# Feed-forward networks that begin by tiles of tokens, and stage boundaries without GpSimd tensor work

## Chip, cores and metric

One NeuronCore of one Trainium2 chip runs the whole program. The metric is the device time of one execution in microseconds (us). Engines are named as the profile names them: PE (TensorE), DVE (VectorE), ACT (ScalarE), POOL (GpSimd), SP (the queue that issues the loads).

## What is computed

Two transformer blocks on 256 tokens of 1024 channels. The first block (two layers of attention, a mixture of experts and a gated embedding, PLE) is touched by the change only at the ends of its PLE stages. The second block is where the change lies:

```
mod = silu(c) @ w_ada + b_ada            # 9 rows of 1024: sh1, sc1, gt1, ...
n = rmsnorm(h, g_ffn1) * (1 + sc1) + sh1
h = h + 0.5 * gt1 * ((silu(n @ w1_gate) * (n @ w1_up)) @ w1_down)     # first feed-forward, D_FF = 2816
n = rmsnorm(h, g_mix) * (1 + sc2) + sh2
h = h + gt2 * hybrid_mixer(n)                                          # mixer
n = rmsnorm(h, g_ffn2) * (1 + sc3) + sh3
h = h + 0.5 * gt3 * ((silu(n @ w2_gate) * (n @ w2_up)) @ w2_down)     # second feed-forward
out = rmsnorm(h, g_final)
```

So each stage needs all of h, its sum of squares per token, a rescaling, and only then its first product.

## The kernel before

The residual h lies in SBUF as two tiles of 128 tokens by 1024 channels (t = 0, 1). Every fp32 product is made of three fp32r products of high and low parts (`mm3`, lines 304 to 306). The parts of a weight are made on the chip: `halves` (line 278) takes a unit of 1 MB, lets ACT copy its high part (line 291) and DVE or POOL subtract it (line 292), in two halves of 128x1024; four slots hold such halves. `self.aside` counts how many of the next halves POOL subtracts in DVE's place: four at the start of each of the three stages of the second block (line 392), one in each PLE stage (line 1411).

Two forms of product are used. `dense` (line 430) has tokens as output rows: 24 matmuls of 512 columns for each tile of tokens and 512 outputs; with `head` or `tail` it finishes tile 0 before tile 1, and then keeps all four halves of the weight until tile 1 has used them. `dense_T` (line 465) has the outputs transposed, with all 256 tokens as columns: 96 matmuls of 256 columns for the same work.

A stage of the second block begins in `modulated_T` (line 387). `rstd` (line 325) squares each half tile on ACT with a running sum (line 334) and takes the reciprocal root in a chain of nine small DVE instructions (lines 337, 314, 316 and 319 with 323 three times). Then `fill` gives PE some products for the modulation rows (`ada`, line 1426, matmuls on line 1447), whose result is copied out of PSUM at once (line 1450). h is transposed by PE (lines 403, 419), 1/rms is transposed and copied (lines 404/405, 420/421), and for each of 8 channel groups DVE scales, ACT adds the shift and rounds, DVE subtracts (lines 409 to 411 by tiles of tokens, the form of the mixer; 425 to 427 for all tokens at once, the form of both feed-forward networks).

`ffn` (line 486) goes through six groups of hidden columns: gate and up by `dense_T`, silu (lines 1523 to 1526), and the product with the down weights one group later, into four PSUM banks (tag a) that it takes at its start. The result reaches h in `add_gated` (lines 1482, 1483), PLE's in lines 1407 to 1409. `finish` multiplies h by the gain on POOL (line 1598), then by 1/rms on ACT and DVE (line 1601), and stores.

Nobody writes out the order by hand: the program order is a priority, and a list scheduler that runs before launch, on its own model of time, fixes each engine's queue and the use of the buffers. `ahead_by(name)` moves work forward in that priority by the number of instructions in `K["hp"]`: rstd 30, silu 200, split 60. The loads sit in SP's queue; nine units of 1 MB can be held.

Of the kernel before, what the change touches and what calls it, by code (L numbers as in the profile page):

```python
# [8 lines left out]
F32 = mybir.dt.float32  # L9
# [7 lines left out]
P = 128  # L17
T = 256
D = 1024
KT = 8  # L20
# [176 lines left out]
class Block:  # L197
    def __init__(self, ctx, tc, A, out, c_at, m_at, s_at, dbg=None):
# [14 lines left out]
        self.flip = 0  # L213
        self.waiting = []
# [109 lines left out]

    def rstd(self, tiles=(0, 1)):
# [3 lines left out]
        with self.ahead_by("rstd"):  # L329
            ss = self.stat([P, n, 2], "ss")  # L330
            for half in range(2):
                for i, t in enumerate(tiles):
                    junk = self.wk.tile([P, 512], BF16, tag="xn", name="junk", bufs=4)
                    nc.scalar.activation(junk, self.h[:, t, half * 512:(half + 1) * 512], AF.Square,
                                         accum_out=ss[:, i, half:half + 1])
            v = self.stat([P, n], "ssv")
            nc.vector.scalar_tensor_tensor(v, ss[:, :, 0], D * EPS, ss[:, :, 1], op0=OP.add, op1=OP.add)
            r = self.stat([P, n], "rstd")
            self.rsqrt(r, v, D)
# [47 lines left out]
    def modulated_T(self, gain, shift, fill, head=False):  # L387

        nc = self.nc
        r = [self.rstd([t]) for t in range(2)]  # L390
        self.fill(*fill)
        self.aside = K["aside"]
        self.fine = bool(K["fmod"])
        with self.ahead_by("mod"):
            hi, lo = self.e([P, KT, T], F32R), self.e([P, KT, T], F32R)
            if head:
                for t in range(2):
                    sl = slice(t * P, (t + 1) * P)
                    ps = [self.psb([P, 4, P]) for _ in range(2)]
# [12 lines left out]
                return hi, lo  # L412
            ps = [self.psb([P, 2, T]) for _ in range(KT // 2)]
            pr = self.psa([P, T])
            rb = self.wk.tile([P, T], F32, tag="xn", name="rbc", bufs=4)
            for t in range(2):
                sl = slice(t * P, (t + 1) * P)
                for kk in range(KT):
                    nc.tensor.transpose(ps[kk // 2][:, kk % 2, sl], self.h[:, t, kk * P:(kk + 1) * P], self.ident)
                nc.tensor.transpose(pr[:, sl], r[t].to_broadcast([P, P]), self.ident)  # L420
                nc.vector.tensor_copy(rb[:, sl], pr[:, sl])
            for kk in range(KT):
                f = self.wk.tile([P, T], F32, tag="xn", name="xn", bufs=4)
                g, b = gain[:, kk:kk + 1], shift[:, kk:kk + 1]
                nc.vector.scalar_tensor_tensor(f, ps[kk // 2][:, kk % 2], g, rb, op0=OP.mult, op1=OP.mult)
                nc.scalar.activation(hi[:, kk], f, AF.Identity, bias=b)  # L426
                nc.vector.scalar_tensor_tensor(lo[:, kk], f, b, hi[:, kk], op0=OP.add, op1=OP.subtract)  # L427
# [968 lines left out]
    def ple(self, i):  # L1396
# [7 lines left out]
        def put(ci, t, ps):  # L1404
# [4 lines left out]
            nc.vector.tensor_tensor(self.h[:, t, sl], self.h[:, t, sl], g, op=OP.add)  # L1409

        self.aside = K["aside_ple"]
# [14 lines left out]
    def ada(self, n, psum):  # L1426
# [23 lines left out]
        self.copy(rows, ps)  # L1450
# [17 lines left out]
    def add_gated(self, i):  # L1468
# [10 lines left out]
        def put(ci, t, ps):  # L1479
# [3 lines left out]
            self.nc.vector.tensor_tensor(self.h[:, t, sl], self.h[:, t, sl], y, op=OP.add)  # L1483
        return put

    def ffn(self, i, name):
        nc = self.nc
        x = self.modulated_T(self.mods[:, 3 * i + 1], self.mods[:, 3 * i], ("ffn", i))
        acc = [[self.psa([P, 512]) for _ in range(2)] for _ in range(2)]
        off, pending, done = 0, None, 0  # L1490
# [20 lines left out]
        for gi, n in enumerate(FF_GROUPS):  # L1511
            both = self.e([P, 2, 4, T], F32R)
            hT = (both[:, 0], both[:, 1])
            banks = []
            for _ in range(2):
                off = self.dense_T(x, name, n, lambda b, ps: banks.append(ps), off)
            self.ada_put()
            nb = n // 2
# [8 lines left out]
            if pending:  # L1527
                down(*pending)
# [138 lines left out]
```

## Time and profile before

| | us |
|---|---|
| median of 3 runs (1133.64 to 1138.91) | 1136.24 |
| the profiled execution, its own time | 1136.35 |
| its span, first to last instruction | 1134.2 |
| PE busy | 1066.5 (94%) |
| DVE busy | 690.4 (61%) |
| ACT busy | 517.9 (46%) |
| POOL busy | 77.2 (7%) |

2.15 us of the profiled execution lie outside its span. "Busy" counts the time in which an engine executes something, at whatever clock; PE's granted clock is a row of its own (1.00 is 2.4 GHz, 0.50 is 1.2 GHz). A row of the timeline gives start, length, engine, line, operation, what it writes and reads, the count of merged instructions, and in brackets how long the engine was idle before, with what ended that.

### The profile page before, as it was taken

To read this page: it belongs to the slowest core of one execution; us is meant where nothing else is said; L and a number is where in the kernel's file an instruction comes from. 1 tells how busy PE (TensorE), PEld (TensorE's weight loads), DVE (VectorE), ACT (ScalarE), POOL (GpSimd) and SP (SyncE) were. 2 spreads that over 40 slices of the span, in tenths; PEclk is the share of its full clock that TensorE was granted. 3 is DMA by queue.
4 is the path that set the end of the run, shared out by engine and by line. 5 is a ranking of instruction groups with operands and counts; after the bars stand their busy time and mean duration, and the time that the engine had idled before them with its cause. 6 is when DMAs were issued, how large, how long until landed. Compare 5 with 4: busy or idle time off the path is not lost.

```text
span 1134.2 us, 18483 instructions
## 1 busy us (share of the span) xinstructions
PE 1066.5 (94%) x7133; PEld 829.5 (73%) x7133; DVE 690.4 (61%) x1672; ACT 517.9 (46%) x995; POOL 77.2 (7%) x61
## 2 busy tenths in 40 slices
PE   7999999999889999899987999999989979999995
PEld 6885547765467667556545999899779659999994
DVE  6696873644479965544367557554675755554555
ACT  5445573422357774231255444343545644444443
POOL 3000000210100002100003000000300030000001
PEclk9998999999999999999998999999999989999998
DMA  9756755789975494799976447755665344454401
GB/s 371 282 203 262 296 223 210 269 340 413 411 300 185 149 382 180 263 386 365 402 277 260 143 159 252 270 179 186 222 270 186 112 185 149 175 186 160 143 26 38
DMA packets 46509, 268.58 MB, mean 237 GB/s; under 512 B 5328, under 2 KB 7120, under 8 KB 20432
## 3 DMA queue, kind: packets, MB, share of 16 engines
q1 hardware_dynamic: 46416, 267.34, 62.3%
q8 instruction: 58, 0.95, 0.3%
q14 instruction: 35, 0.29, 0.1%
HBM read 266.27 MB, written 1.05 MB: 236 GB/s over the span
## 4 chain that ended last, share of the span: by engine, by line
PE 45%; DVE 6%; DMA 1%; ACT 1%; issue 0%; DVEq 0%; ACTq 0%
PE b L305 8%; PE b L304 8%; PE b L306 8%; PE a L304 5%; PE a L306 5%; PE a L305 5%; DVE h L1483 1%; DMA raw<-in_w_ada 1%; PE a L1054 1%; DVE w L1482 1%; PE b L1460 1%; DVE nq L319 1%; PE a L1094 1%; DVE lo L292 0%; PE b L1447 0%; DVE rstd L323 0%
## 5 line engine op out<-in xcount | busy, mean ns | idle before, releaser
L292 DVE TENSOR_TENSOR lo<-raw,hi 128x1024 fp32r<-128x1024 f32 (+2 forms) x220 | 255.6, 1163 | 223.7 <-ACT hi L291 217.9
L291 ACT ACTIVATE hi<-raw 128x1024 fp32r<-128x1024 f32 (+2 forms) x234 | 235.3, 1009 | 284.6 <-PE b L305 143.5
L304 PE MATMUL b<-e,hi 128*128 128x256 f32 x768 | 219.4, 287 | 2.9 <-ACT e L426 2.9
L305 PE MATMUL b<-e,hi 128*128 128x256 f32 x768 | 219.1, 286 | 0.1
L306 PE MATMUL b<-e,lo 128*128 128x256 f32 x768 | 218.6, 285 | 0.0
L305 PE MATMUL a<-lo,e 128*128 128x512 f32 (+2 forms) x512 | 198.2, 388 | 0.0
L304 PE MATMUL a<-hi,e 128*128 128x512 f32 (+2 forms) x512 | 197.0, 393 | 1.2 <-ACT e L410 0.7
L306 PE MATMUL a<-hi,e 128*128 128x512 f32 (+2 forms) x512 | 194.8, 388 | 0.0
L304 PEld LDWEIGHTS b<-e,hi 128*128 128x128 f32 x768 | 149.3, 195 | 4.6 <-ACT e L426 3.5
L305 PEld LDWEIGHTS b<-e,hi 128*128 128x128 f32 x768 | 149.3, 195 | 1.0 <-DVE e L427 0.7
L306 PEld LDWEIGHTS b<-e,lo 128*128 128x128 f32 x768 | 149.1, 194 | 0.0
L304 PEld LDWEIGHTS a<-hi,e 128*128 128x128 f32 x512 | 97.1, 190 | 24.8 <-issue 2.8
L306 PEld LDWEIGHTS a<-hi,e 128*128 128x128 f32 x512 | 96.4, 189 | 20.1 <-DVE e L365 0.8
L305 PEld LDWEIGHTS a<-lo,e 128*128 128x128 f32 x512 | 97.2, 190 | 18.5 <-issue 0.3
L1054 PE MATMUL a<-raw,e 128*32 128x256 f32 x832 | 68.3, 383 | 1.1 <-DVEq L1291 0.8
L1107 PE MATMUL a<-w,GT 128*128 128x512 f32 x128 | 38.4, 419 | 7.7 <-ACT w L1097 3.8
L579 ACT ACTIVATE p<-p,m 128x128 f32<-128x128 f32 (+1 forms) x96 | 42.6, 450 | 6.4 <-DVE m L574 6.2
L1054 PEld LDWEIGHTS a<-raw,e 128*32 128x32 f32 x832 | 28.4, 109 | 23.4 <-issue 5.9
L292 POOL TENSOR_TENSOR lo<-raw,hi 128x1024 fp32r<-128x1024 f32 (+1 forms) x14 | 32.8, 2355 | 160.5 <-ACT hi L291 159.5
L484 DVE TENSOR_TENSOR h<-h,a 128x512 f32<-128x512 f32 x48 | 31.8, 683 | 18.2 <-PE a L1107 12.8
L1033 PE MATMUL b<-G,e 128*128 128x256 f32 x256 | 37.0, 302 | 4.7 <-DVE G L1002 4.6
L1107 PEld LDWEIGHTS a<-w,GT 128*128 128x128 f32 x128 | 21.7, 188 | 26.7 <-ACT w L1097 9.0
(322 smaller groups left out, 1419.1 us busy)
## 6 DMA issues: line engine op xcount, KB each, us to landing
raw<-in_ffn SPq DMA_DIRECT2D x62, 1024.0 KB, 4.8
raw<-in_moe_gu SPq DMA_DIRECT2D x52, 1024.0 KB, 7.4
raw<-in_w_ada SPq DMA_DIRECT2D x36, 1024.0 KB, 5.0
wd<-in_moe_dn SPq DMA_DIRECT2D x64, 512.0 KB, 7.6
raw<-in_w_gate SPq DMA_DIRECT2D x8, 1024.0 KB, 12.8
raw<-in_w_m_in SPq DMA_DIRECT2D x8, 1024.0 KB, 5.6
raw<-in_w_a_in SPq DMA_DIRECT2D x7, 1024.0 KB, 10.4
e<-in_moe_gu SPq DMA_DIRECT2D x6, 1024.0 KB, 10.1
```

The lines of the kernel that those rows point to most:

```text
L291: nc.scalar.activation(hi[:, sl], raw[:, at], AF.Copy)
L292: eng.tensor_tensor(lo[:, sl], raw[:, at], hi[:, sl], op=OP.subtract)
L304: mm(out, l[0], r[0], start=start, stop=False, **kw)
L305: mm(out, l[0], r[1], start=False, stop=False, **kw)
L306: mm(out, l[1], r[0], start=False, stop=stop, **kw)
L319: nc.vector.scalar_tensor_tensor(q, y, h, y, op0=OP.mult, op1=OP.mult)
L484: self.nc.vector.tensor_tensor(self.h[:, t, sl], self.h[:, t, sl], ps, op=OP.add)
L579: nc.scalar.activation(p, p, AF.Exp, bias=m[:, i:i + 1], scale=-1.0, accum_out=den[:, i:i + 1])
L1033: nc.tensor.matmul(ps[:, j], xh[part][:, t, sl], G[:, t], start=(t + j + part == 0), stop=(t + part == 2), skip_group_check=True)
L1054: nc.tensor.matmul(pgs[pp][32 * x:32 * x + 32], xg[:, k, o:o + 32], wg[kk][:, x], start=(k == 0), stop=(k == KT - 1))
L1094: nc.tensor.matmul(py[32 * x:32 * x + 32], hT[:, 32 * x:32 * x + 32], wd[2 * n + x // 2][:, x % 2], start=True, stop=True)
L1107: nc.tensor.matmul(ps, GT[:, t * P:(t + 1) * P], y[:, n * 512:(n + 1) * 512], start=(b == 0), stop=(b == len(back) - 1))
```

## The change

Each rstd of the stage starts and of the end uses sums of squares that are collected when a half tile of h gets its last value. Both feed-forward networks use the norm by tiles of tokens, and compute gate and up of the first group by `dense` with `head`, transposing the product of the silu afterwards. The four accumulator banks are taken one group later. The fill of a stage start comes after tile 0's norm in program order, its results are copied behind the norm, and they lie in the banks of tag a. Nothing is put on POOL in `halves` any more, nor in `finish`. The diff, cut to its core:

```diff
+    def square(self, out, t, half):
+        junk = self.wk.tile([P, 512], BF16, tag="xn", name="junk", bufs=4)
+        self.nc.scalar.activation(junk, self.h[:, t, half * 512:(half + 1) * 512], AF.Square, accum_out=out)
+
+    def square_new(self, ci, t):
+
+        if ci + t == 0:
+            self.squares = self.stat([P, 2, 2], "squares", bufs=1)
+        with self.ahead_by("rstd"):
+            self.square(self.squares[:, t, ci:ci + 1], t, ci)
+
     def rstd(self, tiles=(0, 1)):
...
+            if self.squares is not None:
+                ss = self.squares[:, tiles[0]:tiles[0] + n]
+            else:
...
-    def modulated_T(self, gain, shift, fill, head=False):
-
-        nc = self.nc
-        r = [self.rstd([t]) for t in range(2)]
-        self.fill(*fill)
-        self.aside = K["aside"]
-        self.fine = bool(K["fmod"])
+    def modulated_T(self, gain, shift, fill, head=True):
+
+        nc = self.nc
+        hi, lo = self.e([P, KT, T], F32R), self.e([P, KT, T], F32R)
+        r = [None, None]
         with self.ahead_by("mod"):
-            hi, lo = self.e([P, KT, T], F32R), self.e([P, KT, T], F32R)
             if head:
                 for t in range(2):
                     sl = slice(t * P, (t + 1) * P)
+                    r[t] = self.rstd([t])
+                    if t:
+                        self.squares = None
+                        self.fill(*fill)
                     ps = [self.psb([P, 4, P]) for _ in range(2)]
...
-            ps = [self.psb([P, 2, T]) for _ in range(KT // 2)]
...
+        for rows, ps in self.copies:
+            self.copy(rows, ps)
+        self.copies = []
         return hi, lo
...
             nc.vector.tensor_tensor(self.h[:, t, sl], self.h[:, t, sl], g, op=OP.add)
-
-        self.aside = K["aside_ple"]
+            if i:
+                self.square_new(ci, t)
+
         self.fine = bool(K["fine"])
...
-    def ada(self, n, psum):
+    def ada(self, n, psum, later=False):
...
-        self.copy(rows, ps)
+        if later:
+            self.copies.append((rows, ps))
+        else:
+            self.copy(rows, ps)
...
             self.nc.vector.tensor_tensor(self.h[:, t, sl], self.h[:, t, sl], y, op=OP.add)
+            self.square_new(ci, t)
         return put
...
-        acc = [[self.psa([P, 512]) for _ in range(2)] for _ in range(2)]
...
-            banks = []
-            for _ in range(2):
-                off = self.dense_T(x, name, n, lambda b, ps: banks.append(ps), off)
+            banks, gates, rows = [], [], []
+            nb = n // 2
+            if gi == 0:
+                def put_up(ci, t, ps):
+                    with self.ahead_by("silu"):
+                        f = self.w4([P, 512])
+                        nc.scalar.activation(f, gates[t], AF.Tanh, scale=0.5)
+                        nc.vector.scalar_tensor_tensor(f, f, 1.0, gates[t], op0=OP.add, op1=OP.mult)
+                        nc.vector.scalar_tensor_tensor(f, f, 0.5, ps, op0=OP.mult, op1=OP.mult)
+                        rows.append(f)
+
+                off = self.dense(x, name, [512], lambda ci, t, ps: gates.append(ps), off, head=True)
+                off = self.dense(x, name, [512], put_up, off, head=True)
+                nb = 0
+                for b in range(2):
+                    with self.ahead_by("silu"):
+                        ps = self.psb([P, 2, T])
+                        for j in range(2):
+                            for t in range(2):
+                                nc.tensor.transpose(ps[:, j, t * P:(t + 1) * P],
+                                                    rows[t][:, (2 * b + j) * P:(2 * b + j + 1) * P], self.ident)
+                        self.parts(hT[0][:, 2 * b:2 * b + 2], hT[1][:, 2 * b:2 * b + 2], ps)
+            else:
+                for _ in range(2):
+                    off = self.dense_T(x, name, n, lambda b, ps: banks.append(ps), off)
...
             if pending:
+                if acc is None:
+                    acc = [[self.psa([P, 512]) for _ in range(2)] for _ in range(2)]
                 down(*pending)
...
-                nc.gpsimd.tensor_tensor(o[:, t, sl], self.h[:, t, sl], self.g_final[:, sl], op=OP.mult)
-            for half in range(2):
-                sl = slice(half * 512, half * 512 + 512)
-                self.copy(o[:, t, sl], o[:, t, sl], r)
+                nc.vector.scalar_tensor_tensor(o[:, t, sl], self.h[:, t, sl], r, self.g_final[:, sl], op0=OP.mult,
+                                               op1=OP.mult)
...
-            self.ada(n, self.psb if where.startswith("ffn") else self.psa)
+            self.ada(n, self.psb if where == "ffn0" else self.psa,
+                     where in ("ffn", "mixer"))
```

## Rows read from the trace of the kernel before

**Rows 1.** The page's busy times: us, share of the span, instructions.

```profile
PE 1066.5 (94%) x7133; PEld 829.5 (73%) x7133; DVE 690.4 (61%) x1672; ACT 517.9 (46%) x995; POOL 77.2 (7%) x61
```

**Rows 2.** Engine times by stretch; the last three columns: PE's clock, DMA share, GB/s.

```profile
607.96:620.03 12.07, 5.99 (x40) 2.65 (x40) 10.83 (x28) 4.73 (x11) 5.34 (x2) 0.82 0.91 351
620.03:634.00 13.97, 13.91 (x93) 13.62 (x94) 9.04 (x18) 6.97 (x11) 0.00 (x0) 0.79 0.31 112
817.25:827.76 10.51, 6.40 (x50) 2.78 (x50) 10.12 (x28) 4.38 (x11) 5.15 (x2) 0.98 0.97 386
827.76:842.04 14.28, 14.28 (x64) 11.95 (x65) 10.85 (x36) 8.99 (x19) 0.00 (x0) 0.90 0.56 228
919.75:931.66 11.91, 5.70 (x34) 2.69 (x33) 10.57 (x29) 4.78 (x12) 5.26 (x2) 0.78 0.88 353
931.66:945.50 13.84, 13.79 (x95) 13.49 (x96) 9.37 (x18) 6.96 (x11) 0.00 (x0) 0.82 0.15 48
1122.80:1134.20 11.40, 0.00 (x0) 0.00 (x0) 7.32 (x24) 3.15 (x8) 3.38 (x3) 0.72 0.25 92
```

**Rows 3.** Timeline, second PLE stage into the first feed-forward network.

```profile
605.34 7.96 POOL L292 TENSOR_TENSOR lo<-raw,hi 128x1024 fp32r<-128x1024 f32 x3 [0.34 <-ACT hi L291]
...
606.68 1.62 DVE L1408 SCALAR_TENSOR_TENSOR w<-w,e 128x512 f32<-128x512 f32 x1 [5.18 <-ACT w L1407]
...
607.89 2.77 PE L1447 MATMUL b<-raw,c 128*32 128x512 f32 x22
...
608.33 2.75 DVE L1409 TENSOR_TENSOR h<-h,w 128x512 f32<-128x512 f32 x1
...
611.61 2.24 DVE L1408 SCALAR_TENSOR_TENSOR w<-w,e 128x512 f32<-128x512 f32 x1
...
613.88 0.69 DVE L1409 TENSOR_TENSOR h<-h,w 128x512 f32<-128x512 f32 x1
...
614.50 0.15 DVE L337 SCALAR_TENSOR_TENSOR ssv<-ss 128x1 f32<-128x1 f32 x1
...
614.61 0.63 ACT L334 ACTIVATE junk<-h 128x512 bf16<-128x512 f32 x1 [1.67 <-DVE h L1409]
...
615.15 0.19 ACT L334 ACTIVATION_READ_ACCUMULATOR junk<-h 128x1 f32 x1
...
616.09 0.16 DVE L323 SCALAR_TENSOR_TENSOR rstd<-nq,rstd 128x1 f32<-128x1 f32 x1
...
616.81 0.29 DVE L421 COPY rbc<-a 128x128 f32<-128x128 f32 x1 [0.19 <-PE a L420]
...
618.96 1.27 DVE L425 SCALAR_TENSOR_TENSOR xn<-b,mods,rbc 128x256 f32<-128x256 f32 x3
...
620.04 0.58 PE L304 MATMUL b<-e,hi 128*128 128x256 f32 x1 [1.45 <-ACT e L426]
```

**Rows 4.** Timeline, first feed-forward network into the mixer.

```profile
813.27 0.69 DVE L1482 TENSOR_TENSOR w<-a,w 128x512 f32<-128x512 f32 x1 [5.29 <-PE a L306]
...
818.74 2.67 DVE L1483 TENSOR_TENSOR h<-h,w 128x512 f32<-128x512 f32 x1
```

**Rows 5.** Timeline of DVE, mixer into the second feed-forward network.

```profile
918.12 1.29 DVE L1482 TENSOR_TENSOR w<-a,w 128x512 f32<-128x512 f32 x2 [5.53 <-PE a L306]
...
923.33 2.83 DVE L1483 TENSOR_TENSOR h<-h,w 128x512 f32<-128x512 f32 x2
```

**Rows 6.** The chain that ended last: start, us, what (a step's pitch).

```profile
585.15 0.87 PE b L359 x8
...
605.24 0.23 PE a L304
...
638.71 0.12 PE b L305
```

**Rows 7.** DVE by line and form from 600 us on: count, busy us, mean ns.

```profile
L292 DVE TENSOR_TENSOR lo<-raw,hi 128x1024 fp32r<-128x1024 f32 x137 | 167.8, 1225 | 156.5 <-ACT hi L291 156.0
```

**Rows 8.** Timeline, the end of the program.

```profile
1130.01 0.72 ACT L261 ACTIVATE e<-e,rstd 128x512 f32<-128x512 f32 x1 [0.84 <-DVE rstd L323]
```

More of the change, by code (lines that the diff above doesn't have):

```diff
@@ L329, in rstd @@
         with self.ahead_by("rstd"):
-            ss = self.stat([P, n, 2], "ss")
-            for half in range(2):
[L332 to L335, printed above, removed]
+            if self.squares is not None:
+                ss = self.squares[:, tiles[0]:tiles[0] + n]
+            else:
+                ss = self.stat([P, n, 2], "ss")
+                for half in range(2):
+                    for i, t in enumerate(tiles):
+                        self.square(ss[:, i, half:half + 1], t, half)
             v = self.stat([P, n], "ssv")
@@ L398, in modulated_T @@
                     sl = slice(t * P, (t + 1) * P)
+                    r[t] = self.rstd([t])
+                    if t:
+                        self.squares = None
+                        self.fill(*fill)
                     ps = [self.psb([P, 4, P]) for _ in range(2)]
@@ L411, in modulated_T @@
                         nc.vector.scalar_tensor_tensor(lo[:, kk, sl], f, b, hi[:, kk, sl], op0=OP.add, op1=OP.subtract)
-                return hi, lo
-            ps = [self.psb([P, 2, T]) for _ in range(KT // 2)]
[L414 to L427, printed above, removed]
+        for rows, ps in self.copies:
+            self.copy(rows, ps)
+        self.copies = []
         return hi, lo
@@ L1488, in ffn @@
         x = self.modulated_T(self.mods[:, 3 * i + 1], self.mods[:, 3 * i], ("ffn", i))
-        acc = [[self.psa([P, 512]) for _ in range(2)] for _ in range(2)]
-        off, pending, done = 0, None, 0
+        off, pending, done, acc = 0, None, 0, None
         n_tiles = sum(FF_GROUPS)
@@ L1513, in ffn @@
             hT = (both[:, 0], both[:, 1])
-            banks = []
-            for _ in range(2):
-                off = self.dense_T(x, name, n, lambda b, ps: banks.append(ps), off)
+            banks, gates, rows = [], [], []
[22 more added lines that the diff above has]
+                    off = self.dense_T(x, name, n, lambda b, ps: banks.append(ps), off)
             self.ada_put()
-            nb = n // 2
             for b in range(nb):
@@ L1597, in finish @@
                 sl = slice(half * 512, half * 512 + 512)
-                nc.gpsimd.tensor_tensor(o[:, t, sl], self.h[:, t, sl], self.g_final[:, sl], op=OP.mult)
-            for half in range(2):
-                sl = slice(half * 512, half * 512 + 512)
-                self.copy(o[:, t, sl], o[:, t, sl], r)
+                nc.vector.scalar_tensor_tensor(o[:, t, sl], self.h[:, t, sl], r, self.g_final[:, sl], op0=OP.mult,
+                                               op1=OP.mult)
                 nc.sync.dma_start(self.out[t * P:(t + 1) * P, sl], o[:, t, sl])
```

## The prediction, made before the changed kernel was run

> **What bounds the kernel now.** I read the page's busy times first, then the engine times by stretch, then the timeline at each stage boundary, and last the chain that ended last. PE is busy 94% of the span [rows 1], so away from the boundaries only fewer or faster matmuls would help. The reader should see in the stretches that the boundaries are where it is not so. From PE's last product of one stage to its first of the next pass 12.07 us (second PLE into first feed-forward, called P), 10.51 us (into the mixer, M) and 11.91 us (into the second feed-forward, F), of which PE works 5.99, 6.40 and 5.70; after PE's last product 11.40 us remain (E) [rows 2]. The stretch behind each boundary, up to the end of its first weight matrix, runs at a mean clock of 0.79, 0.90 and 0.82 of 2.4 GHz: it begins at 1.2 GHz. What that loses is length times what is missing of 1: 13.97 x 0.21 = 2.9, 14.28 x 0.10 = 1.4, 13.84 x 0.18 = 2.5 us. The three boundaries so hold 6.1 + 4.1 + 6.2 = 16.4 us of PE idle and 6.8 us of lost clock.
>
> What fills them is the chain last product, h final, squares, reciprocal root, norm, first product. In it DVE is stretched while POOL subtracts weights: in P three instructions of 512 columns take 1.62, 2.75 and 2.24 us during POOL's 7.96, and the next, when POOL has ended at 613.30, takes 0.69 [rows 3]. In M one takes 2.67 [rows 4], with 5.15 us of POOL in that stretch [rows 2].
>
> **The parts.** Each boundary is rebuilt with the prices of [rows 3]: a DVE instruction of 512 columns 0.69 us; a square 0.63 and its read of the sum 0.19, 0.82; the root from 614.50 to 616.25, 1.75; up to the end of the copied 1/rms at 617.10, 0.85 more; from the norm's first instruction at 618.96 to the first product at 620.04, 1.1. (What lies between 617.10 and 618.96 is the second tile's root, which tile 0 need not await when the norm goes by tiles.) From a tile's squares to its first product that is 3.7 us.
>
> P. DVE does tile 0's last two instructions from 606.68 to 608.06. Tile 0's sum would be ready at 608.9; I take 609.5, since ACT has tile 1's tanh to give at the same time, and 0.5 more because the root shares DVE with tile 1's last instructions. First product at 609.5 + 0.5 + 3.7 = 613.7 instead of 620.04 [rows 3].
>
> The first matrix then goes by tiles as the mixer's does now: 14.28 us [rows 2], less 1.4 for the clock and less 16 matmuls for modulation rows that the mixer has inside (about 0.1 each, 1.6) makes 11.3. To that I add 1.2 for one weight half that DVE must now subtract while the norm needs it. End 626.2 instead of 634.00: **-7.8**.
>
> M. The norm is by tiles already. DVE needs 4 x 1.38 from 813.27, done at 818.8 instead of 821.41 [rows 4]. Tile 0's chain would allow a product near 821.8; but PE has work of its own: 32 matmuls of the fill from 817.25 at 0.126 (2.77 / 22 [rows 3]), 4.0, and eight transposes, 0.87 [rows 6]. That gives about 822.3 instead of 827.76: -5.5. With PE filled I expect no fall of the clock, -1.4; one subtraction in the way, +1.2. **-5.7**.
>
> F. DVE cannot start before 918.12, when the accumulations end nearly together [rows 5]. Three pairs of instructions end tile 0 at 922.3, its square ends at 923.1, plus 3.7 is 926.8, or 927.3 with the same 0.5 as in P; I take 927.0 against 931.66. PE has only 14 matmuls of the fill and transposes for that time, so I leave the clock low: 11.3 + 1.4 + 1.2 = 13.9, end 940.9 instead of 945.50 [rows 2]. **-4.6**.
>
> E. The last update of h starts at 1122.85, after PE's last product [rows 2]: 1.38, square 0.82, root 1.75, two scalings on DVE at 0.69 each make 1128.2; the last instruction now ends at 1130.73 [rows 8]. -2.5, less 0.5 for tile 0's root and scaling on the same DVE: **-2.0**. The stores behind it stay.
>
> What the change adds. Sixteen transposes of the silu product per network, 16 x 0.109 [rows 6] = 1.7. Up by tiles takes 48 x 0.23 = 11.0 rather than 96 x 0.12 = 11.5 [rows 6], -0.5 (gate's is in the sums above). **+2.4** for both networks. POOL's twelve subtractions of the second block cost DVE 12 x 1.23 [rows 7] = 14.7 us. Two of each four lie before the boundary, where DVE waits 5.18, 5.29 and 5.53 us for PE [rows 3 to 5]; of the others I charged one. Without that cover it would be two more per boundary, 2.5 us. The halves moved from POOL in PLE and half of the squares hide beside the products of the stage before.
>
> Edits that I cost at nothing: the copies of the fill move behind the norm (each of the price of an instruction of 512 columns at most), and what reads them, the modulation rows, waits till the first group is done; their PSUM banks are wanted next by up, eleven us after gate begins. SP's queue keeps the order of its loads, since the fill's still stand before the stage's weights; in M, where DMA is at 0.97, the first units have landed by the time of their subtraction. The accumulators move behind the first group and are first used in the second. No row shows a head pass in a network, nor two in a row; bounds: nothing, since the mixer's goes over into the next matrix at 842.04 without idle [rows 2], or a subtraction and its copy on ACT, 2.4 us, at each of four handovers, 10 us. I take nothing, the nearest row being the mixer's.
>
> **Sum.** 7.8 + 5.7 + 4.6 + 2.0 - 2.4 = 17.7. The profiled execution took 1136.35, 0.11 over the median of the runs, so this makes 1118.6. The most that the rows hold is all idle and all lost clock, 23.2, and 2.5 in E, less 2.4: 23.3, or 1113; two more for E and for stores that wait less, and the range ends at 1111.
>
> **A rule that speaks against it.** In P the clock fell between PE's last transposes and the first product: the boundary as a whole has 0.82, the stretch behind it 0.79 [rows 2], after 22 fill matmuls and then mostly transposes. The Trainium skill (TensorE: Matmul & The Clock Gate, Part 4: PE-mode transpose) says that transposes do not count as PE activity for the clock. By that rule the fill of my gaps with transposes would not hold the clock in P and M; no row here separates the two. That mechanism is rival 3.
>
> **Rivals.**
> 1. *DVE becomes the bound.* It is busy 10.83 of 12.07 us in P, 10.12 of 10.51 in M, 10.57 of 11.91 in F [rows 2]. Against it: in P 4.5 of that is stretch (6.61 less 3 x 0.69), and tile 1's root, about 2, may come after tile 0's first products, so 4.3 remain, or 5.6 with one subtraction, in the 5.7 us that I leave. For it: that is no room at all, and if the second subtraction or tile 1's root stand first, 1.2 to 2 us go at each start and as much again in the norm. I price it as half of the gain: (17.7 + 2.4) / 2 - 2.4 = 7.7, 1128.7.
> 2. *Split slots (slower).* Head passes hold all four slots of split halves until tile 1's pass. If the next matrix's halves come only after that pass, each takes ACT and then DVE (1.23 [rows 7], and ACT about as much), 2.4, where PE uses one in 6 x 0.23 = 1.4 [rows 6]: per handover 2.4 for the first and 1.0 for each of three more, 5.4, plus 1.4 for the silu's two DVE instructions at the same time; four handovers, 27 us: 1145.6. Against: the mixer hands over to its second matrix without idle (PE 14.28 of 14.28 [rows 2]). It decides from 4.4 us a handover on (17.7 / 4).
> 3. *Low clock at all three starts.* The fall that I remove in P and M stays: 2.9 + 1.4 = 4.3, 1122.9.
> 4. *The order eats it.* The scheduler's queues are fixed ahead on its own model: PE's may hold tile 1's transposes before tile 0's products, DVE's a subtraction before the puts, and other stages may shift. Then tiles first does not happen, and what the missing POOL gives is paid for by the moved subtractions: about 0 to -3, 1134.5.
>
> **Chances.** Forecast 0.52; rival 1 0.19; rival 3 0.14; rival 4 0.08; rival 2 0.07. A measurement of this kernel can tell about 0.5%, 5.7 us, from no change: 1130.5 to 1142. The forecast, rivals 1 and 3 lie below: 0.85. Rival 4 is no change, 0.08; rival 2 is slower, 0.07. To leave out no more than two in ten the range must take in rival 1 with its bounds (one unit of splitting more, 2.5): 1111 to 1131.
>
> **What would show it.** No POOL rows at line 292 or 1598; lines 1409 and 1483 at 0.69 throughout; boundary stretches, from PE's last product to its first, of about 5.7, 5.0 and 7.3 us where they are 12.07, 10.51 and 11.91. The clock behind P and M near 1.00 and behind F near 0.9. Gate and up of the first group without PE idle. Tile 0's first products ahead of tile 1's transposes in PE's timeline. I am wrong if PE idles at the handovers from gate to up, or if DVE's rows between the stages show no waiting while PE does, or if the stages before the second PLE change length.

## The result, and the profile after

The changed kernel takes 1121.6 us, the median of 4 runs (1121.3 to 1122.49); beside it the kernel before took 1137.58. The ratio is 0.9864, with a 95% interval of 0.9842 to 0.9886: faster by 1.4%, 3.0 us less than forecast and inside the range. A second series of six runs gave 1121.43 and 0.9855 (0.9825 to 0.9885).

The page's busy times after, which answer to [rows 1]:

```profile
PE 1057.6 (95%) x6957; PEld 815.0 (73%) x6957; DVE 694.9 (62%) x1720; ACT 520.1 (46%) x1009; POOL 38.9 (3%) x43
```

The engine times by stretch of the changed kernel, columns as in [rows 2]. The borders are PE's last and first main products (0.1 to 0.2 us ahead of those in [rows 2]): P, the first network, M, the mixer, F, the second network, E. In what follows a stretch between two stages is a wait, and the stage behind it a body.

```profile
605.86:616.96 11.10, 7.42 (x47) 2.65 (x47) 10.59 (x40) 5.84 (x14) 0.00 (x0) 0.85 0.61 222
616.96:810.77 193.81, 193.81 (x1297) 177.71 (x1298) 119.04 (x148) 86.62 (x107) 1.90 (x2) 1.00 0.61 218
810.77:821.54 10.77, 7.71 (x51) 3.15 (x50) 10.42 (x40) 6.33 (x15) 0.00 (x0) 0.84 0.56 206
821.54:910.79 89.25, 87.73 (x505) 73.25 (x505) 52.52 (x142) 46.28 (x79) 0.00 (x0) 1.00 0.49 180
910.79:921.00 10.21, 5.83 (x35) 3.31 (x35) 10.02 (x34) 4.96 (x13) 0.00 (x0) 0.83 0.57 207
921.00:1109.21 188.21, 188.21 (x1249) 173.68 (x1249) 107.80 (x135) 85.81 (x108) 0.00 (x0) 1.00 0.39 137
1109.21:1119.14 9.93, 0.17 (x1) 0.00 (x0) 6.61 (x25) 1.45 (x4) 0.00 (x0) 0.71 0.28 106
```

The three waits have hardly become shorter: 11.10, 10.77 and 10.21 us, where 5.7, 5.0 and 7.3 were forecast. What became shorter is the bodies behind them. Both networks have PE busy for their whole length at a clock of 1.00, and the low clock (0.85, 0.84, 0.83 in the mean) now lies inside the waits: in P it was 1.2 GHz from about 616 to 626 us before, and is so from about 612 to 615 us after, over by the first product. Cut in the same places, the profile before has 12.25 + 197.04, 10.68 + 91.91, 11.99 + 190.96 and 11.60 us. So a wait with its body got 4.38, 2.57 and 4.53 us shorter, E 1.67. The 1.93 that is left of the 15.1 lies ahead of P. Some 1.2 of it is ten of the fill's 32 products, which before ran among PLE's products (from 588.70 us on) and now stand in the wait; the rest is less than the scatter there: the kernels below whose stages up to P are alike reach it between 604.2 and 610.6 us.

What PE and DVE do in P, from the timeline after:

```profile
606.98 0.69 DVE L1410 SCALAR_TENSOR_TENSOR w<-w,e 128x512 f32<-128x512 f32 x1
...
607.73 1.23 DVE L294 TENSOR_TENSOR lo<-raw,hi 128x1024 fp32r<-128x1024 f32 x1
...
608.12 0.19 ACT L329 ACTIVATION_READ_ACCUMULATOR junk<-h 128x1 f32 x1
...
608.87 0.68 DVE L1411 TENSOR_TENSOR h<-h,w 128x512 f32<-128x512 f32 x1
609.47 0.15 DVE L351 SCALAR_TENSOR_TENSOR ssv<-squares 128x1 f32<-128x1 f32 x1
...
609.70 0.63 PE L418 MATMUL b<-consts,h 128*128 128x128 f32 x4 [1.43 <-DVE ssv L351]
611.40 0.32 PE L419 MATMUL a<-consts,rstd 128*128 128x128 f32 x1 [1.06 <-DVE rstd L325]
611.65 5.30 PE L1450 MATMUL a<-raw,c 128*32 128x512 f32 x32
616.89 0.32 PE L419 MATMUL a<-consts,rstd 128*128 128x128 f32 x1
616.96 0.48 PE L306 MATMUL a<-hi,e 128*128 128x512 f32 x1
```

DVE's instructions of 512 columns take 0.69 instead of 1.62 to 2.75 [rows 3]. Tile 0's sum of squares is read out by 608.31, but its root begins at 609.47, since DVE has a weight subtraction (607.73) and tile 1's last update in front of it: 3.6 us behind PE's last product, where the prediction had 1.5 and 0.5 more (609.5 with that product at 607.96). PE, besides, has left its 32 products of the fill (line 1450, nothing the network waits for) until tile 0's transposed 1/rms is through, and runs them at 611.65, mostly at the low clock (0.69 in the mean from 611.40 to 616.96), while the first product (line 306) stands behind them in its queue. In [rows 3] 22 of them ran at 607.89, inside the idle time. In M it is the same:

```profile
815.94 0.32 PE L419 MATMUL a<-consts,rstd 128*128 128x128 f32 x1 [1.57 <-DVE rstd L325]
816.20 5.34 PE L1450 MATMUL a<-raw,c 128*32 128x512 f32 x32
...
821.54 0.47 PE L306 MATMUL a<-hi,e 128*128 128x512 f32 x1
```

The update of h in the kernel before, DVE by line and form (count, busy us, mean ns of one, idle time before them):

```profile
L1483 DVE TENSOR_TENSOR h<-h,w 128x512 f32<-128x512 f32 x12 | 15.8, 1320 | 0.2
L1482 DVE TENSOR_TENSOR w<-a,w 128x512 f32<-128x512 f32 x12 | 8.1, 684 | 16.1 <-PE a L306 16.1
```

and after:

```profile
L1489 DVE TENSOR_TENSOR h<-h,w 128x512 f32<-128x512 f32 x12 | 8.2, 688 | 0.2
L1488 DVE TENSOR_TENSOR w<-a,w 128x512 f32<-128x512 f32 x12 | 8.1, 685 | 5.3 <-PE a L308 5.3
```

Only the addition was stretched, 1320 ns against 688; the product beside it, which reads one operand from PSUM, took 684 and 685. The Trainium skill (SBUF — State Buffer, Who interferes with whom) says that a DVE instruction with two SBUF inputs contends with a GpSimd instruction that reads SBUF; these rows agree.

### The profile page after: what moved, and what is told of

Same layout as the page of the kernel before. It is cut to its first block, busy times and chain, and to the rows that moved or that the text cites. A ratio compares the mean times of both kernels' runs of the same rounds, so it can differ in the third digit from the quotient of the medians.

```text
span 1119.1 us, 18152 instructions
## 1 busy us (share of the span) xinstructions
PE 1057.6 (95%) x6957; PEld 815.0 (73%) x6957; DVE 694.9 (62%) x1720; ACT 520.1 (46%) x1009; POOL 38.9 (3%) x43
## 4 chain that ended last, share of the span: by engine, by line
PE 46%; DVE 4%; DMA 1%; ACT 1%; issue 0%; DVEq 0%
PE b L306 7%; PE b L307 7%; PE b L308 7%; PE a L306 6%; PE a L308 6%; PE a L307 6%; DVE lo L294 1%; PE a L1450 1%; DMA raw<-in_w_ada 1%; PE a L1056 1%; DVE h L1489 1%; DVE w L1488 1%; PE b L1466 1%; ACT hi L293 1%; PE a L1096 0%
## 5 line engine op out<-in xcount | busy, mean ns | idle before, releaser
L294 DVE TENSOR_TENSOR lo<-raw,hi 128x1024 fp32r<-128x1024 f32 (+2 forms) x234 | 271.3, 1162 | 227.2 <-ACT hi L293 221.0
L307 PE MATMUL a<-lo,e 128*128 128x512 f32 (+2 forms) x576 | 222.0, 387 | 0.0
L306 PE MATMUL a<-hi,e 128*128 128x512 f32 (+2 forms) x576 | 220.6, 391 | 0.5 <-ACT e L378 0.3
L308 PE MATMUL a<-hi,e 128*128 128x512 f32 (+2 forms) x576 | 218.5, 388 | 0.0
L306 PE MATMUL b<-e,hi 128*128 128x256 f32 x640 | 181.8, 284 | 0.0
L307 PE MATMUL b<-e,hi 128*128 128x256 f32 x640 | 181.4, 283 | 0.0
L308 PE MATMUL b<-e,lo 128*128 128x256 f32 x640 | 181.2, 283 | 0.0
L306 PEld LDWEIGHTS a<-hi,e 128*128 128x128 f32 x576 | 108.8, 189 | 24.5 <-issue 1.9
L308 PEld LDWEIGHTS a<-hi,e 128*128 128x128 f32 x576 | 108.3, 189 | 21.6 <-issue 0.8
L306 PEld LDWEIGHTS b<-e,hi 128*128 128x128 f32 x640 | 123.0, 192 | 1.1 <-ACT hi L293 0.8
L307 PEld LDWEIGHTS a<-lo,e 128*128 128x128 f32 x576 | 108.8, 189 | 20.6 <-issue 0.3
L307 PEld LDWEIGHTS b<-e,hi 128*128 128x128 f32 x640 | 123.0, 192 | 0.3
L308 PEld LDWEIGHTS b<-e,lo 128*128 128x128 f32 x640 | 122.9, 192 | 0.0
L1096 PE MATMUL a<-wd,hT 128*32 128x512 f32 x256 | 41.1, 617 | 1.5 <-ACT hT L1091 1.2
```

What stands on the lines that cost most here:

```text
L294: eng.tensor_tensor(lo[:, sl], raw[:, at], hi[:, sl], op=OP.subtract)
L306: mm(out, l[0], r[0], start=start, stop=False, **kw)
L307: mm(out, l[0], r[1], start=False, stop=False, **kw)
L308: mm(out, l[1], r[0], start=False, stop=stop, **kw)
L1096: nc.tensor.matmul(py[32 * x:32 * x + 32], hT[:, 32 * x:32 * x + 32], wd[2 * n + x // 2][:, x % 2], start=True, stop=True)
```

## The experiments

Time is compared by the ratio to the kernel before on the same chip. Where it went is read from one profiled execution each, by the seven stretches (wait + body, us). The rows with a plus, both orders and one held have the fill first besides.

| kernel | P + network | M + mixer | F + network | E | sum | median | ratio (95%) |
|---|---|---|---|---|---|---|---|
| before | 12.25 + 197.04 | 10.68 + 91.91 | 11.99 + 190.96 | 11.60 | 526.4 | 1137.58 | 1 |
| changed | 11.10 + 193.81 | 10.77 + 89.25 | 10.21 + 188.21 | 9.93 | 513.3 | 1121.60 | 0.9864 (0.9842, 0.9886) |
| before, no GpSimd | 9.01 + 196.97 | 7.42 + 90.54 | 10.14 + 190.78 | 9.91 | 514.8 | 1124.09 | 0.9882 (0.9853, 0.9911) |
| GpSimd back | 12.88 + 193.79 | 14.18 + 88.35 | 12.32 + 188.19 | 9.92 | 519.6 | 1127.19 | 0.9905 (0.9869, 0.9941) |
| all tokens | 8.83 + 195.89 | 10.71 + 89.25 | 11.14 + 190.35 | 9.92 | 516.1 | 1125.67 | 0.9886 (0.9858, 0.9913) |
| fill first | 7.68 + 193.80 | 7.42 + 89.34 | 9.63 + 188.21 | 9.92 | 506.0 | 1116.81 | 0.9821 (0.9790, 0.9851) |
| fill first, again | 7.67 + 193.79 | 7.41 + 89.31 | 9.62 + 188.21 | 9.92 | 505.9 | 1119.08 | 0.9813 (0.9781, 0.9845) |
| + squares late | 13.79 + 196.18 | 13.71 + 89.00 | 15.85 + 190.25 | 9.92 | 528.7 | 1138.22 | 0.9988 (0.9968, 1.0008) |
| + copies at once | 7.67 + 195.41 | 7.42 + 89.34 | 9.71 + 189.59 | 9.93 | 509.1 | 1118.65 | 0.9818 (0.9788, 0.9849) |
| + DVE's order | 8.34 + 195.94 | 7.24 + 90.26 | 9.70 + 190.48 | 9.92 | 511.9 | 1118.75 | 0.9813 (0.9783, 0.9843) |
| root's bank | 7.93 + 196.25 | 8.93 + 90.95 | 9.93 + 189.09 | 9.94 | 513.0 | 1123.48 | 0.9864 (0.9833, 0.9896) |
| both orders | 5.88 + 197.77 | 6.36 + 91.32 | 7.52 + 190.85 | 9.92 | 509.6 | 1118.07 | 0.9812 (0.9784, 0.9839) |
| one held | 5.88 + 197.38 | 6.36 + 89.48 | 8.96 + 189.59 | 9.92 | 507.6 | 1114.64 | 0.9797 (0.9767, 0.9827) |

**The fill first.** The fill's products come ahead of the norm in program order, as before the change:

```diff
         r = [None, None]
+        self.fill(*fill)
         with self.ahead_by("mod"):
...
                         self.squares = None
-                        self.fill(*fill)
```

> The changed kernel with the fill put at the head of modulated_T, ahead of tile 0's norm in program order; its copies stay behind the norm. Theory (the fill's products, which now stand in PE's queue behind tile 0's transposed 1/rms, cost 5.3, 5.3 and 1.9 us there while PE idled 4 to 5 us before): first products come some 3.7 us earlier in P, 3.8 in M, 0.5 in F, the clock in P stays high; about 6 us less than the changed kernel, 1115 to 1117 us. Rival (the norm on DVE sets the pace anyway, the fill only filled time that the norm needs): under 2 us, 1120 to 1122.

The theory held: 1116.81, and the waits shrink by 3.4, 3.4 and 0.6 us (in P 0.9 of that is eight of the fill's products, which now run ahead of the border). The timeline of P:

```profile
605.52 2.78 PE L1450 MATMUL a<-raw,c 128*32 128x512 f32 x24
608.24 2.10 PE L418 MATMUL b<-consts,h 128*128 128x128 f32 x16
611.49 0.29 PE L419 MATMUL a<-consts,rstd 128*128 128x128 f32 x1 [1.15 <-DVE nq L321]
612.97 0.29 PE L419 MATMUL a<-consts,rstd 128*128 128x128 f32 x1 [1.19 <-ACT e L425]
613.10 0.47 PE L306 MATMUL a<-hi,e 128*128 128x512 f32 x1
```

The fill now lies where PE has nothing else, and the first product comes 7.7 us behind the last one; the prediction had 5.7 (613.7 behind 607.96). Tile 1's transposed root still stands ahead of it in PE's queue, which the prediction had not.

**GpSimd alone, both ways.** The kernel before without tensor work on GpSimd, and the changed kernel with the weight subtractions of the stage starts back on it:

```diff
-    aside=4,
+    aside=0,
...
-    aside_ple=1,
+    aside_ple=0,
```

and the gain of the last norm on DVE as in the change;

```diff
         r = [None, None]
+        self.aside = K["aside"]
...
+        self.aside = K["aside_ple"]
         self.fine = bool(K["fine"])
```

> The kernel before, with all subtractions and the final gain on VectorE and nothing else changed. Theory (GpSimd's stretching of VectorE is the larger part of what the change removes): 8 to 12 us faster than the kernel before, 1126 to 1130. Rival (the parts by tiles and by earlier squares carry the gain): 0 to 4 us faster, 1134 to 1138.

> The changed kernel with the first four weight halves of each stage of the second block, and one of each PLE stage, subtracted on GpSimd again (the end stays on VectorE). Theory (GpSimd stretches VectorE's two-operand instructions at the boundaries by some 4 us each, and VectorE takes the subtractions mostly in idle time): 7 to 11 us slower than the changed kernel, 1129 to 1133. Rival (VectorE is the bound at the boundaries, so what it gains without GpSimd it pays for the subtractions): within 2 us, 1120 to 1124.

The first came out below its theory's 1126: taking GpSimd away from the kernel before gives 13.4 us by the ratio, where the whole change gives 15.5 (0.0118 and 0.0136 of 1138.5), and 11.7 of 13.2 by the stretches. Its P and M:

```profile
606.62:615.63 9.01, 5.63 (x42) 2.64 (x41) 8.31 (x29) 4.62 (x11) 0.00 (x0) 0.94 0.96 394
...
812.60:820.02 7.42, 6.32 (x52) 2.79 (x51) 7.22 (x28) 3.91 (x9) 0.00 (x0) 1.00 0.76 282
```

Both waits are shorter than the changed kernel's. In the kernel before, the first product of all three stages waits for the norm (ACT's e, 0.70 to 1.45 us), not for a weight half, which points to the stretch of DVE's chain and not to GpSimd's own pace. The fill first, run on the same chip, is 7.3 us below this kernel (1116.81): the rest of the change is worth that much where the fill stays early, and 1.5 to 2 where it is late. Put back, GpSimd costs 5.6 us by the medians, 4.7 by the ratios and 6.4 by the stretches, between the two theories; the timeline shows the stretched instruction again (L1411 here is L1410 of the changed kernel):

```profile
605.44 5.10 POOL L294 TENSOR_TENSOR lo<-raw,hi 128x1024 fp32r<-128x1024 f32 x2
605.65 2.70 DVE L1411 SCALAR_TENSOR_TENSOR w<-w,e 128x512 f32<-128x512 f32 x1 [2.42 <-ACT w L1410]
```

The two sizes, 13.4 and 5.6, differ because the parts don't add: in E the gain of 1.7 stays in the second kernel (its last norm is not put back), and its low clock lies in the waits (0.73, 0.76, 0.72) while its bodies stay at 1.00. How much is due to each, no run separates.

**All tokens.** The networks' norm and first group for all 256 tokens at once, as before the change; the rest as changed (`head=False`, and `dense_T` for the first group).

> The changed kernel with both feed-forward networks' norm and first group for all tokens at once as before (GpSimd, squares, copies and accumulators stay as changed; the fill of the networks then stands ahead of the transposes again). Theory of the prediction (tiles first let the first product start early): 4 to 8 us slower than the changed kernel, 1126 to 1130. Rival (in the changed kernel the late fill ate that head start, and the sixteen transposes cost 1.7 us per network): within 2 us of it, or faster, 1118 to 1123.

1125.67 lies between the two. By the ratio it is 0.0022 slower than the changed kernel, which the intervals don't separate; by the stretches 2.8 us, all of it at F (3.1). At P it costs nothing (-0.2), since that form of norm also brings the fill forward (8.83). So in the kernel as changed, tiles first is worth some 3 us, and loses at P what the fill's place takes. Beside the fill first, which ran on the same chip and has the fill early in the networks too, it is worth more: 3.2 us at P and 3.7 at F by the stretches, in which 3.2 more lie at M, where this kernel is as changed; the medians are 8.9 us apart and the intervals don't meet.

**Where the fill's place comes from.** One word of the changed kernel: the transposed 1/rms goes into a bank of the transposes' pool.

```diff
-                    pr = self.psa([P, P])
+                    pr = self.psb([P, P])
```

> The changed kernel with one word altered: tile 0's and tile 1's transposed 1/rms go into a bank of the other PSUM pool (the one the transposes use), not into the pool that the modulation products and the network's products share. Theory (the products of the fill stand behind tile 0's transposed 1/rms because PSUM banks of a pool are handed out in program order, so that they wait for the bank that follows it): the fill's products move ahead of it in TensorE's order by themselves, the gaps between main products shrink from 11.1, 10.8 and 10.2 us to 7 to 8.5 at P, 7 to 8.5 at M and 9 to 10 at F, and the time falls 5 to 8 us below the changed kernel's 1121.6. Rival (it is the place in the program, which sets the priority): order and gaps stay, 1120 to 1123.

At P and F the gaps came as the theory has them, at M 0.4 longer (8.93); the time, at the changed kernel's ratio, did not. In P:

```profile
605.02 3.63 PE L1450 MATMUL a<-raw,c 128*32 128x512 f32 x30
...
611.35 0.29 PE L419 MATMUL b<-consts,rstd 128*128 128x128 f32 x1 [2.11 <-DVE nq L321]
611.48 1.20 PE L418 MATMUL b<-consts,h 128*128 128x128 f32 x8
...
612.85 0.50 PE L306 MATMUL a<-hi,e 128*128 128x512 f32 x1 [0.17 <-ACT e L425]
```

Nothing but the pool of that small tile was changed, and the fill begins 0.1 us behind the last product instead of 5.8 (605.02 after 604.92, 611.65 after 605.86): sharing a pool with the fill and the products is what held it. That banks are handed out in program order is the reading that fits; no run shows the handing out itself. The waits give back 5.3 us, and the bodies take 5.0: the products begin while tile 0's norm is still going, and at a clock of 0.98 to 0.99 in two bodies.

**Late squares, and copies at once,** both on top of the fill first: `square_new` does nothing; and `ada` is always called with `later` False.

> The kernel with the fill's products first, with the squares summed only where the 1/rms is wanted, as before the change. Theory (two squares of 0.63 us and a read of 0.19 each stand on ScalarE in front of tile 0's root, behind weight conversions of 1.05): 0.5 to 1.5 us more at each of P, M and F, and 0 to 2 at E, so 2 to 5 us more than with the early squares, 1119 to 1122. Rival (VectorE's order ends each wait later than the squares do, whichever place they have): every gap within 0.4 us, the time within 1 us of 1116.8.

> The kernel with the fill's products first, with the fill's copies issued right behind them, as before the change, not behind the norm. Theory (with the fill early, its copies are ready in the idle part of the wait and are taken there anyway): every gap within 0.7 us, the time within 1.5 us of 1116.8. Rival (copies of 0.68 us stand ahead of the root on VectorE or of the squares on ScalarE): 0.7 to 1.4 us more at P and M and 0.7 at F, 1119 to 1121.

Late squares cost far more than either theory: 1138.22, all of the change's gain. The timeline of P shows why:

```profile
620.98 0.40 ACT L425 ACTIVATE e<-xn,mods 128x128 fp32r<-128x128 f32 x1 [0.39 <-DVE xn L424]
...
621.28 0.61 ACT L329 ACTIVATE junk<-h 128x512 bf16<-128x512 f32 x1
...
621.90 0.61 ACT L329 ACTIVATE junk<-h 128x512 bf16<-128x512 f32 x1
...
624.67 0.45 PE L419 MATMUL a<-consts,rstd 128*128 128x128 f32 x1 [7.42 <-DVE rstd L325]
...
624.79 0.76 PE L306 MATMUL a<-hi,e 128*128 128x512 f32 x1
```

Tile 1's squares (line 329) stand on ACT behind seven of tile 0's eight normed blocks (line 425), its root follows them, and PE, in order, idles 7.42 us for that root with tile 0's products queued behind. So in this order, with tile 1's root queued ahead of the first product, the early squares are what lets a start by tiles work; their own 0.82 us are the small part. Late squares with that root behind the first products were not run. E is 9.92 either way: there they are worth nothing. The copies' place is worth nothing that these runs show: the waits are the same to 0.1 us, and so is the ratio to 0.0003.

**What keeps the waits above the forecast.** On top of the fill first, tile 1's root waits for tile 0's, and two weight subtractions and the fill's copies wait for four of tile 0's eight blocks (`issue_after`):

```diff
-                    r[t] = self.rstd([t])
+                    with self.tc.issue_after(self.root.ins) if t else nullcontext():
+                        r[t] = self.rstd([t])
...
-                    eng.tensor_tensor(lo[:, sl], raw[:, at], hi[:, sl], op=OP.subtract)
+                    with self.behind():
+                        eng.tensor_tensor(lo[:, sl], raw[:, at], hi[:, sl], op=OP.subtract)
```

> The kernel with the fill's products first, and besides it three things held back on VectorE at the three starts: tile 1's root until tile 0's is done, and two weight subtractions (1.22 us each) and the fill's copies (0.68) until four of tile 0's eight normed blocks are out. Theory (what keeps those gaps at 7.67, 7.41 and 9.64 us is VectorE's other work ahead of tile 0's root: 1.9 us of it at P, about 3 at M, 1.2 to 2.4 at F, and 0.6 of interleaved roots at each): gaps of 5.3 to 6.3 at P, 4.7 to 5.8 at M and 7.0 to 8.5 at F, the bodies of the stages unchanged, a span of 1104 to 1108 against 1111.4. Rival (the subtractions held back starve the first products, or another chain such as ScalarE's is as long): gaps or bodies give it back, span 1110 to 1113.

The theory fell: the waits are 8.34, 7.24 and 9.70, the bodies 5.3 longer in sum. Tile 0's transposed root came 4.6 us behind the last product (605.92) instead of 6.1, and P became longer all the same, 8.34. In this kernel and the two that follow, the lines have other numbers: L316 and L318 are main products, L432 the transposed root, L296 the weight subtraction, L270 the copy, L439 the norm's subtraction, L335 the root's last step. PE's timeline in P, with that step:

```profile
610.53 0.27 PE L432 MATMUL a<-consts,rstd 128*128 128x128 f32 x1
...
613.91 0.15 DVE L335 SCALAR_TENSOR_TENSOR rstd<-nq,rstd 128x1 f32<-128x1 f32 x1
...
614.21 0.29 PE L432 MATMUL a<-consts,rstd 128*128 128x128 f32 x1 [3.41 <-ACT e L438]
...
614.26 0.47 PE L316 MATMUL a<-hi,e 128*128 128x512 f32 x1
```

PE waits 3.41 us for tile 1's root, delayed by the edit itself and ahead of the first product in the queue (the bracket names ACT, but the root ended at 614.06). Both orders together:

> The fill's products first, the three things held back on VectorE as in the run of the vector order, and the transposed 1/rms of each tile in a bank of the transposes' pool as in the run of the root's bank. Theory (in the run of the vector order TensorE's queue held tile 1's transposed root ahead of the first product, which idled 3.41 us for it; the other bank puts that root behind the first products): the first product follows tile 0's root by about 2 us, gaps of 5.8 to 6.8 at P, 5.0 to 6.5 at M and 7.8 to 9.0 at F. The bodies are 193.8, 89.3 and 188.2 us where the clock doesn't fall and up to 2.5 more each where it falls behind the wait; so a span of 1105 to 1113, and 2 to 5 us less than the kernel with the fill's products alone first. Rival (tile 1's root, now inside the products, stops TensorE there for as long, or the clock falls at all three starts whatever the gap): the bodies give it all back, and the time is within 1.5 us of that kernel's or above it.

The gaps are those of the theory or shorter (5.88, 6.36, 7.52), 5.0 us less in sum than with the fill first; the bodies are 8.6 longer, and the time is the rival's: 1118.07, beside 1119.08 for the fill first on the same chip. One reason is a stop that the edit makes, the two held subtractions and a copy ahead of tile 0's fifth block on DVE (the next expectation calls it the seventh), and PE at that block:

```profile
612.68 2.35 DVE L296 TENSOR_TENSOR lo<-raw,hi 128x1024 fp32r<-128x1024 f32 x2
614.95 0.68 DVE L270 COPY w<-a 128x512 f32<-128x512 f32 x1
615.55 0.33 DVE L439 SCALAR_TENSOR_TENSOR e<-xn,mods,e 128x128 fp32r<-128x128 f32 x1
...
615.94 0.50 PE L318 MATMUL a<-hi,e 128*128 128x512 f32 x1 [1.50 <-DVE e L439]
```

So one subtraction only was held, behind six blocks (`2, 2` becomes `3, 1`, `kk == 3` becomes `kk == 5`), with the changed kernel beside it on the same chip:

> As the run of both orders, but only one weight subtraction is held back, and it and the fill's copies wait for six of tile 0's eight normed blocks, not four. Theory (in that run the two subtractions and a copy, 2.35 and 0.68 us, stood before tile 0's seventh block and stopped TensorE there: 1.50, 1.50 and 0.90 us of idle behind P, M and F, and slower products around them): gaps of 5.8 to 6.2 at P, 6.5 to 7.5 at M and 8.0 to 9.0 at F, bodies without those stops, a span of 1106 to 1112, and 1 to 4 us less than the run of both orders. Rival (VectorE's whole work for the norm of both tiles sets when the second tile's products can run, wherever the one subtraction stands): the idle moves to the second tile's products and the time stays within 1 us of 1118.1.

> The changed kernel itself beside the run above, on the same chip. By its first runs 1121.3 to 1122.5 with a clock of 0.985 to 0.988, a span of 1119.1 made of gaps of 11.1, 10.8 and 10.2 us and bodies of 193.8, 89.2 and 188.2: theory (its fall of the clock always lands on the fill, in the waits) the same again, 1120.5 to 1123.5, a spread under 2 us; rival (its falls reach the products in other executions, as those of the other kernels do): a spread of 4 us or more.

1114.64 (1114.0 to 1117.22) against 1121.43 (1120.5 to 1124.21): 6.8 us under the changed kernel, 22.4 under the one before: the lowest median and ratio of all, though its interval (0.9767 to 0.9827) takes in the fill first (0.9821 and 0.9813). The gaps are the theory's at P and F and 0.1 shorter at M. The changed kernel repeated itself, five of six runs within 1.4 us and one 3.7 above the lowest, between theory and rival, with its fall of the clock in the waits again (0.84, 0.84, 0.83). The stop in P is 0.52, in M none:

```profile
610.49:807.87 197.38, 196.34 (x1297) 178.67 (x1297) 123.75 (x167) 88.10 (x113) 1.90 (x2) 0.99 0.59 213
...
814.23:903.71 89.48, 87.95 (x505) 73.21 (x505) 57.21 (x161) 48.05 (x86) 0.00 (x0) 1.00 0.49 186
```

In P the first product is 1.8 us earlier than with the fill first, yet wait and body together are 1.8 longer. The traces say where that went. The 96 products of gate and up end 29.3 us behind PLE's last product, against 29.7 with the fill first, both at a clock of 1.00: 1.4 of the lead went to products that came at the norm's pace on DVE. Then PE stops at the silu's transposes, where the fill first does not:

```profile
634.41 0.44 PE L1555 MATMUL b<-consts,w 128*128 128x128 f32 x2 [0.52 <-DVE w L1544]
```

and from about 637 to 640 us its clock is 1.2 GHz (0.56 in the mean from 636.80 to 640.50), which costs some 1.6 us more.

**The fill first, again,** to see whether its clock of 1.00 holds:

> The kernel with the fill's products first once more, beside the run above. In its first profile the granted clock was 1.00 behind all three waits; its nearest neighbour, with the copies at once, has the same gaps and falls at P and F. Theory (whether the clock falls behind such a wait is chance between executions): gaps of 7.6 to 7.8, 7.3 to 7.6 and 9.5 to 9.8 again, but a low clock behind at least one of the three starts, a body or two longer by 1 to 2.5 us, median 1116 to 1119. Rival (this order of the work keeps the clock up): 1.00 in all three again, bodies of 193.8, 89.3 and 188.2, median 1113 to 1116.

Its profile repeats the first to 0.1 us. But its six executions ran at mean clocks of 0.980 to 0.993 and spans of 1110.2 to 1120.3 us, with the median, 1119.08, at the theory's upper edge: the profile is as the rival has it, the median as the theory has it. Both profiles show the good end. The stretches above are to be read as where time can go, the medians as what it takes.

## Why the prediction was right, and where its steps failed

Sign and range held; 1121.6 lies 3.0 us above the forecast and 1.3 below rival 3's 1122.9. The way there did not hold, and that the number came so near is in part luck. The three waits were to give 16.5 us and gave 2.8; the bodies were to grow by 0.8, the added transposes included, and shrank by 8.6; and 1.9 lie ahead of P. The stages before the second PLE kept their length: its first tanh begins at 596.89 us before, at 596.53 and 597.14 in the two profiles after. By stretches, in us (the +2.4 for the added transposes shared equally between the networks):

| | forecast | changed | fill first | one held |
|---|---|---|---|---|
| P and first network | -6.6 | -4.38 | -7.81 | -6.03 |
| M and mixer | -5.7 | -2.57 | -5.83 | -6.75 |
| F and second network | -3.4 | -4.53 | -5.11 | -4.40 |
| E | -2.0 | -1.67 | -1.68 | -1.68 |

- **The step that failed is the fill's place.** In M the prediction wrote that PE has 32 matmuls of the fill from the last product on, and in P it took the chain of tile 0's root alone. In the changed kernel they run behind that root, for 5.30 and 5.34 us. Put ahead again, wait and body together reach the forecast at both.
- **The chain of tile 0's root was too short as well.** In P the prediction let it begin 2.0 us behind PE's last product; with the fill first it begins 4.1 behind (609.48 after 605.42), behind a copy, a subtraction and tile 1's update on DVE. So with the fill first the waits stay 2.0, 2.4 and 2.3 us above the forecast (7.68, 7.42, 9.63 against 5.7, 5.0, 7.3), and the sums come out because the bodies give more than was forecast.
- **GpSimd.** That DVE's three instructions shrink to 0.69 was right to the hundredth. But the prediction credited the gain to the new chain as a whole; taken alone, this one part gives 11.7 of the 13.2 us, and the rest of the change nets 1.5 by the stretches, because the fill's place costs up to 7.3 (513.3 less 506.0; 5 to 6 by the ratios).
- **Tile 0's products ahead of tile 1's transposes** did not come: PE holds tile 1's transposes and root ahead of the first product. This is what rival 4 named, with a subtraction ahead of the puts, which came too (607.73 in P); its price, the whole gain, was wrong.
- **The clock.** Forecast near 1.00 behind P and M and 0.9 behind F; it is 1.00 behind all three. Yet it fell in all three waits, as rival 3 has it, and took its price from the fill: 5.30 us for 32 products where 24 take 2.78, so 3.7 at full clock. Rival 3's 1122.9 is near the time, by another way.
- **Rival 2** is excluded: PE is busy 193.81 of 193.81 us from the first gate product on, handovers included. The silu's added transposes don't show either: 190.96 less the 2.5 us of lost clock was 188.5, and is 188.21.
- **Rival 1** came in part. The prediction's own sign against itself was DVE without waiting while PE waits, and DVE is busy 10.59 of 11.10, 10.42 of 10.77 and 10.02 of 10.21 us of the waits. In P its chain holds PE until 611.40; from there to the first product PE is busy with the fill. Where PE was let in earlier it stopped for DVE's blocks.
- **E** came at its size, though from the gain's move off GpSimd alone: E is 9.91 in the kernel before without GpSimd, with squares summed late. Up to the last scaling E is 1.2 us shorter, not 2.0: tile 1's root takes 2.96 us instead of 1.75, since tile 0's scalings (1.41) lie in it on DVE. The stores behind, which the prediction left as they were, are 0.5 shorter.
- **Costed at nothing:** the copies held in a run of their own; accumulators and SP's order were not taken apart, but PE idles nowhere in the networks. The early squares were priced at 0.82 us a tile, and without them the kernel with the fill first gains nothing (0.9988).

## What to carry to other kernels

Look first at which instructions are stretched while another engine runs: taking that cause away alone gave 11.7 of the 13.2 us (1.7 of it in E, where the last norm's product changed its form as well). When work is moved in program order to hide it, read the new queue order of the engine that must stay in order; here a fill placed later in the program, with one small tile ahead of it in a PSUM pool that they share, pushed 5.3 us of idle-time work in front of the first product. A start by tiles needs everything of the second tile (squares, root, transposes) either done early or queued behind the first tile's products, and an earlier first product pays only as far as the vector engine's blocks keep up.

## What was not expected of the hardware

The granted clock fell or not behind the same order of work. With the fill first, F's wait ran at 1.00; with only the copies' place changed and PE's rows in it the same, at 0.80:

```profile
903.66:913.29 9.63, 4.95 (x35) 2.38 (x34) 9.44 (x32) 4.92 (x13) 0.00 (x0) 1.00 0.97 370
```

```profile
906.55:916.26 9.71, 5.71 (x35) 2.78 (x35) 9.52 (x32) 4.92 (x13) 0.00 (x0) 0.80 0.96 359
```

The Trainium skill (TensorE: Matmul & The Clock Gate, Part 4: PE-mode transpose) says that transposes in PE's transpose mode do not count as PE-busy in the same way. These runs neither show nor exclude it: the same transposes were followed by both levels. In the second execution the clock fell 6 us into the wait, behind 16 products of the fill, four transposes, a pause of 2 us and eight more transposes, which stand alike in the first. What decides between the levels in waits of 7 to 10 us stays open.
